# Block products for sixteen unit pairs of both FFNs, their weight sums made by accumulating transfers

## The chip, the cores and the metric

The kernel runs on one core of a Trainium2 chip. The metric is the device time of one execution in microseconds; three runs of the kernel before gave a median of 1001.37 us. A profile comes from one further execution of its own, traced by the hardware profiler.

## What is computed

One decoder layer on a sequence of 512 tokens with 1024 features: a half-step SwiGLU FFN, a token mixer (eight stick-breaking heads and eight forgetting-attention heads), and a second half-step SwiGLU FFN. Each is normed, and shifted, scaled and gated by columns that come from the vector c. Cut to what matters here (everything is float32):

```
mod = silu(c) @ w_mod + b_mod            # nine vectors of 1024: shift, scale, gate of each sub-layer
h = rms_norm(x, g1) * (1 + sc1) + sh1
x = x + 0.5 * (1 + ga1) * ((silu(h @ w1_gate) * (h @ w1_up)) @ w1_down)     # D_FF = 2816
x = x + (1 + ga2) * hybrid_mixer(...)
h = rms_norm(x, g2) * (1 + sc3) + sh3
x = x + 0.5 * (1 + ga3) * ((silu(h @ w2_gate) * (h @ w2_up)) @ w2_down)
```

## The kernel before

Everything is held transposed: features on the 128 partitions, the 512 tokens along the free dimension. x is eight tiles of 128x512, h likewise. Matmuls run in fp32r on operands that are split in two: a high part (a cast, on ACT, `hi`) and the rest (a subtraction, on VectorE, `lo`). A product of a 128x128 weight block with an activation tile takes three matmuls (`mm3`): high by high, high by low, low by high.

**The FFN.** D_FF is 22 units of 128. A plain unit has a gate and an up projection, each of eight 128x128 blocks, so 24 matmuls of 512 columns into one PSUM bank. `gated` makes silu(gate) * up from them and splits it into `ah` and `al`. The units come in three parts (`FPARTS`, 8, 7 and 7); after each part `down` multiplies the part's activations with eight chunks of the down weights (bank `pt`) and `update` adds the gated result to x. Weights go through `prep`: a transfer on SyncE's queue into a `raw` slot (4 slots of 512 KB), the cast into `hi` (4 slots), the subtraction into `lo` (4 slots). A slot of hi or lo comes free when the product that reads it is done, so the split of one operand can run when the product four earlier has ended.

**The block pair** (`block_pair`). For seven pairs of neighbouring units of the second FFN (`SPLIT2`) the gate and up projections of two units are taken as one 2x2 block matrix product in the Strassen-Winograd form: seven products of half-size blocks in place of eight. The host stores the four quarter blocks (d11, d12, d21, d22, each 128x1024) of a pair one after another. Each product has 24 matmuls of 256 columns: two halves of four blocks by three. Four of the seven weight operands are sums of quarter blocks:

```
s1 = d21 + d22      s2 = s1 - d11      s3 = d11 - d21      s4 = d12 - s2
```

VectorE makes them from the raw tiles into `bsum` tiles (L458), and they are split like the others (L452, L453). The matching sums of h are made once (`block_sums`, L418 to L440): four of 256 tokens wide for each pair of h tiles, split into `th` and `tl`. The results are put together by VectorE (`result`, L480) in `bres` tiles (6 slots); the first product stays in its bank and is also copied out by ACT (L486). The order of the products is d11, s2, s1, d12, s3, s4, d22. Three banks are used: `o` for d11 and d12, `mm` and `z` for the rest.

**The modulation columns.** The 72 columns of 128 come from chunks of 128x1024 of w_mod, read into `wm` tiles (4 slots). VectorE multiplies a chunk with c and sums it into one column of `mods` (L215), and then adds the bias column (L218). The first 16 are made at the start. The other 56 are queued: `mod_next` takes two after each of the units 4 to 7 of the first FFN, three after each later one, and one after each down chunk.

**The end of the first FFN.** In the last part, five down chunks are done in full, `SumSq` collects the squares of x on GpSimd (L625), and three chunks are held back, split into `bw` tiles of their own, for `turn`, which finishes x and makes the next h in two halves of the tokens so that TensorE goes on.

**The order of the work.** Apart from stretches that are written out by hand (the start, and TensorE's order around the two turns), each engine's queue is put in order when the program is built, from the order of the code as priority and from estimated durations; at run time every queue is worked off in that order, SyncE's queue of loads included. A tile is handed out from the slots of its tag, and a load or an operation that writes it waits until the last reader of the slot's tile before is done. GpSimd issues no transfers. Outside of the turns its queue in the two FFNs is empty.

## Time and profile before

| | |
|---|---|
| runs, median (lowest) | 1001.37 us (1000.51 us) |
| the profiled execution's own time | 1001.51 us |
| its span, first to last instruction | 999.6 us |
| granted TensorE clock | 0.998 |
| TensorE / weight loads / VectorE / ACT / GpSimd busy | 984.3 / 847.7 / 666.4 / 401.8 / 117.9 us |
| read from HBM | 125.92 MB |

The stages, by the lines in the trace: the start and the first four units until about 60 us, the first FFN until its turn at some 370 us, the mixer until 645 us, the second FFN to the end. The block pairs stand between 680.3 and 936 us.

A row of a group or of the timeline names the line of the code, the engine, the operation and the tiles (out<-in, buffer numbers left out). In the timeline a row begins with its start and its duration. PEld is the loading of weights, which overlaps PE. What an engine waited for stands as `waiting line <- engine and line that released it`. TensorE pipelines its matmuls, so the distance of two starts, and not the duration, tells how fast they follow each other.

### The profile page before, as it was taken

The numbers are of one execution on the slowest core, as the hardware profiler recorded it, in microseconds if no ns is written. First come the engines' busy times: TensorE is split into PE (matmuls) and PEld (weight loads), VectorE is DVE, ScalarE is ACT, GpSimd is POOL, SyncE is SP. The second block draws the span as 40 slices with busy tenths as digits, with TensorE's granted clock in tenths as the row PEclk, the third lists the DMA queues.
The fourth block names the chain that finished last, engine by engine and source line by source line (L and its number), as shares of the span: only waits on it lengthen the run. The fifth ranks groups of instructions, "written<-read, shape, count | busy, mean of one in ns | idle before, by whom it ended". The sixth has DMA issues, their size and how long they took to land.

```text
span 999.6 us, 14256 instructions
## 1 busy us (share of the span) xinstructions
PE 984.3 (98%) x5648; PEld 847.7 (85%) x5648; DVE 666.4 (67%) x1042; ACT 401.8 (40%) x628; POOL 117.9 (12%) x131
## 2 busy tenths in 40 slices
PE   8999999999999999998999999999999999999998
PEld 7888788888888899877887867999988999899987
DVE  7999988524333437688767686699755678467532
ACT  6342222322223326587557462465431445134420
POOL 2000000000000033065413335110000000000000
PEclk9999999999999999999999999999999999999999
DMA  9888899432222402311111111213242224323321
GB/s 362 317 299 326 319 336 330 148 93 103 105 92 88 138 16 92 127 64 43 64 64 64 43 44 64 85 62 118 84 140 85 85 85 130 103 85 106 114 87 52
DMA packets 37362, 128.94 MB, mean 129 GB/s; under 512 B 4400, under 2 KB 4656, under 8 KB 37296
## 3 DMA queue, kind: packets, MB, share of 16 engines
q1 hardware_dynamic: 35712, 125.88, 36.4%
q10 hardware_dynamic: 1584, 2.16, 0.6%
q8 instruction: 44, 0.72, 0.3%
q14 instruction: 22, 0.18, 0.1%
HBM read 125.92 MB, written 2.10 MB: 128 GB/s over the span
## 4 chain that ended last, share of the span: by engine, by line
PE 81%; DVE 9%; issue 3%; ACT 3%; DMA 3%; POOL 1%; SPq 0%; ACTq 0%; DVEq 0%; POOLq 0%
PE mm L129 8%; PE pt L130 7%; PE pt L131 7%; PE pt L129 7%; PE mm L130 7%; PE mm L131 7%; PE z L131 4%; PE z L130 4%; PE z L129 4%; PE mm L475 2%; PE mm L474 2%; PE mm L473 2%; DMA wm<-wmod 2%; PE o L1019 2%; PE mm L401 1%
## 5 line engine op out<-in xcount | busy, mean ns | idle before, releaser
L124 ACT CAST hi<-raw 128x1024 fp32r<-128x1024 f32 (+2 forms) x126 | 129.1, 1027 | 287.0 <-PE pt L130 105.1
L125 DVE TENSOR_TENSOR lo<-raw,hi 128x1024 fp32r<-128x1024 f32 (+2 forms) x125 | 151.6, 1214 | 74.4 <-ACT hi L124 72.0
L129 PE MATMUL mm<-hh,hi 128*128 128x512 f32 (+1 forms) x352 | 136.1, 387 | 0.0
L130 PE MATMUL mm<-hl,hi 128*128 128x512 f32 (+1 forms) x352 | 134.1, 381 | 0.1
L131 PE MATMUL mm<-hh,lo 128*128 128x512 f32 (+1 forms) x352 | 134.0, 381 | 0.0
L130 PE MATMUL pt<-al,hi 128*128 128x512 f32 (+1 forms) x331 | 128.2, 387 | 0.6 <-DVE al L414 0.6
L129 PE MATMUL pt<-ah,hi 128*128 128x512 f32 (+1 forms) x331 | 128.1, 387 | 0.0
L131 PE MATMUL pt<-ah,lo 128*128 128x512 f32 (+1 forms) x331 | 128.0, 387 | 0.0
L569 DVE SCALAR_TENSOR_TENSOR x<-pt,gcol,x 128x512 f32<-128x512 f32 (+1 forms) x51 | 36.3, 712 | 100.0 <-PE pt L131 99.9
L130 PE MATMUL z<-hl,hi 128*128 128x512 f32 (+1 forms) x224 | 83.7, 374 | 0.0
L131 PE MATMUL z<-hh,lo 128*128 128x512 f32 (+1 forms) x224 | 83.7, 374 | 0.0
L129 PE MATMUL z<-hh,hi 128*128 128x512 f32 (+1 forms) x224 | 83.7, 374 | 0.0
L129 PEld LDWEIGHTS mm<-hh,hi 128*128 128x128 f32 x352 | 66.5, 189 | 13.8 <-issue 2.2
L131 PEld LDWEIGHTS mm<-hh,lo 128*128 128x128 f32 x352 | 66.4, 189 | 12.9
L130 PEld LDWEIGHTS mm<-hl,hi 128*128 128x128 f32 x352 | 66.5, 189 | 12.3 <-DVE hl L169 0.3
L215 DVE SCALAR_TENSOR_TENSOR junk<-wm,c_bc 128x1024 f32<-128x1024 f32 x56 | 68.3, 1219 | 11.8 <-DMA wm<-wmod 11.7
L130 PEld LDWEIGHTS pt<-al,hi 128*128 128x128 f32 x331 | 62.2, 188 | 13.6 <-DVE al L414 0.9
L129 PEld LDWEIGHTS pt<-ah,hi 128*128 128x128 f32 x331 | 62.2, 188 | 12.8 <-ACT ah L413 0.2
L131 PEld LDWEIGHTS pt<-ah,lo 128*128 128x128 f32 x331 | 62.2, 188 | 12.5
L625 POOL TENSOR_TENSOR sqp<-x 128x512 f32<-128x512 f32 x10 | 11.3, 1134 | 351.5 <-DVE x L569 351.5
L410 DVE TENSOR_TENSOR av<-sg,z 128x512 f32<-128x512 f32 x27 | 18.5, 685 | 48.8 <-PE z L131 48.8
L130 PEld LDWEIGHTS z<-hl,hi 128*128 128x128 f32 x224 | 42.2, 188 | 7.5
(349 smaller groups left out, 2159.6 us busy)
## 6 DMA issues: line engine op xcount, KB each, us to landing
raw<-w SPq DMA_DIRECT2D x80, 512.0 KB, 3.6
wm<-wmod SPq DMA_DIRECT2D x72, 512.0 KB, 5.8
raw<-wqk SPq DMA_DIRECT2D x16, 512.0 KB, 3.6
raw<-w1d SPq DMA_DIRECT2D x16, 448.0 KB, 3.2
raw<-w2d SPq DMA_DIRECT2D x16, 448.0 KB, 3.3
raw<-w1s SPq DMA_DIRECT2D x8, 512.0 KB, 5.7
raw<-w1d SPq DMA_DIRECT2D x8, 512.0 KB, 5.2
raw<-wo SPq DMA_DIRECT2D x8, 512.0 KB, 3.4
```

What stands on the lines that cost most here:

```text
L124: nc.scalar.copy(hi, raw)
L125: (lo_engine or nc.vector).tensor_tensor(lo, raw, hi.bitcast(F32), op=ALU.subtract)
L129: nc.tensor.matmul(ps, lh, rh, start=first, stop=False)
L130: nc.tensor.matmul(ps, lh, rl, start=False, stop=False)
L131: nc.tensor.matmul(ps, ll, rh, start=False, stop=last)
L215: nc.vector.scalar_tensor_tensor(out=junk, in0=wm, scalar=1.0, in1=c_bc, op0=ALU.mult, op1=ALU.mult, accum_out=mods[:, i : i + 1])
L410: nc.vector.tensor_tensor(av[:, sl], sg[:, sl], u, op=ALU.mult)
L473: nc.tensor.matmul(b[:, sl], lh, rh, start=f, stop=False, skip_group_check=True)
L474: nc.tensor.matmul(b[:, sl], lh, rl, start=False, stop=False, skip_group_check=True)
L475: nc.tensor.matmul(b[:, sl], ll, rh, start=False, stop=e, skip_group_check=True)
L569: nc.vector.scalar_tensor_tensor(out=x[e][:, sl], in0=ps[:, sl], scalar=g_col(gm)[:, e : e + 1], in1=x[e][:, sl], op0=ALU.mult, op1=ALU.add)
L1019: nc.tensor.matmul(ob[g * 64 : g * 64 + 64, i * P : (i + 1) * P], V[:, i + j, (2 * p + g) * 64 : (2 * p + g + 1) * 64], pts[g][0][:, at + ...
```

## The change

- **More pairs.** `SPLIT2` is now every second unit from 4 to 20 (nine pairs), and the first FFN gets `SPLIT1`, every second unit from 8 to 20 (seven pairs), its weights stored by the host in the same way. `FPARTS` becomes 8, 8, 6, so that no pair straddles two parts. In the first FFN `block_sums` is called after the first part.
- **Sums by transfers.** The four sums of weight blocks are made by transfers that GpSimd issues and that add what they bring to what lies in the destination. s1 is d21 loaded and d22 added. s2 and s3 change their signs: ACT writes the negated tile (of s1, and of d11), and a transfer adds d11 or d21 from HBM, so they are d11 - s1 and d21 - d11. The fourth is made in the buffer of d12, once d12 has been split for its own product: s2 is added to it, from SBUF. So d11, d21 and d22 are each read twice.
- **Signs and order.** `block_sums` forms its second and third sum with the opposite sign. The order of the products becomes d11, s1, s2, d12, s3, s4, d22.
- **Buffers.** The negated tiles take slots of `wm`, which they share with the modulation chunks and with `block_sums`. `th` and `tl`, the squares at the start and the weights held back for `turn` share eight tiles `tb0` to `tb7`. `bres` has 4 slots, and `SumSq`, `turn` and the start of the first FFN take their tiles from it too.
- **Modulation columns.** The bias is added once for eight columns. `mod_next` takes one chunk after a pair of the first FFN and two after each down chunk.

The core of the diff:

```diff
-FPARTS = (8, 7, 7)
-SPLIT2 = (3, 6, 8, 11, 13, 15, 18)
+FPARTS = (8, 8, 6)
+SPLIT1 = tuple(range(8, NF, 2))
+SPLIT2 = tuple(range(4, NF, 2))
...
-        nc.vector.tensor_tensor(mods[:, i : i + 1], mods[:, i : i + 1], cols[:, i : i + 1], op=ALU.add)
...
             if d < KD - 1:
                 continue
+            nc.vector.tensor_tensor(mod_col(m), mod_col(m), cols[:, m * KD : (m + 1) * KD], op=ALU.add)
...
     def block_tile(tmp):
-        return tmp.tile([P, 2 * S], F32, tag="bsum", name=nm("bsum"), bufs=3)
+        return tmp.tile([P, 2 * S], F32, tag="wm", name=nm("bsum"), bufs=4)
...
-            nc.vector.tensor_tensor(t3, b1, a1, op=ALU.subtract)
-            nc.vector.tensor_tensor(t2, t3, a0, op=ALU.add)
-            nc.vector.tensor_tensor(t4, b0, t2, op=ALU.subtract)
-            hi = tmp.tile([P, 2 * S], F32R, tag=f"th{k}", name=nm("th"), bufs=1)
-            lo = tmp.tile([P, 2 * S], F32R, tag=f"tl{k}", name=nm("tl"), bufs=1)
+            nc.vector.tensor_tensor(t3, a1, b1, op=ALU.subtract)
+            nc.vector.tensor_tensor(t2, t3, a0, op=ALU.subtract)
+            nc.vector.tensor_tensor(t4, b0, t2, op=ALU.add)
+            hi = tmp.tile([P, 2 * S], F32R, tag=f"tb{2 * k}", name=nm("th"), bufs=1)
+            lo = tmp.tile([P, 2 * S], F32R, tag=f"tb{2 * k + 1}", name=nm("tl"), bufs=1)
...
     def block_pair(w, n_w, j, T, tmp):
-        raws = []
-        for n in range(4):
+        d11, d12, d21, d22 = (w[n_w + n] for n in range(4))
+
+        def load(src):
             raw = wpool.tile([P, 2 * S], F32, tag="raw", name=nm("raw"), bufs=4)
-            nc.sync.dma_start(raw, w[n_w + n])
-            raws.append(raw)
-        r11, r12, r21, r22 = raws
+            nc.sync.dma_start(raw, src)
+            return raw
+
+        def add_in(dst, src):
+            nc.gpsimd.dma_start(dst, src, accum_op=ALU.add)
+
+        def negated(src, other):
+            t = block_tile(tmp)
+            nc.scalar.mul(t, src, -1.0)
+            add_in(t, other)
+            return t
+
+        s1 = load(d21)
+        add_in(s1, d22)
+        r11 = load(d11)
...
-        def combined(x0, x1, op):
-            t = block_tile(tmp)
-            nc.vector.tensor_tensor(t, x0, x1, op=op)
-            return t
...
-                out = tmp.tile([P, S], F32, tag="bres", name=nm("bres"), bufs=6)
+                out = tmp.tile([P, S], F32, tag="bres", name=nm("bres"), bufs=4)
...
         bx, by, bz = bank("o"), bank("mm"), bank("z")
-        product(bx, parts(r11), whole_h(0, H0), True, True)
-        p1 = tmp.tile([P, S], F32, tag="bres", name=nm("bres"), bufs=6)
+        s2 = negated(s1, d11)
+        s3 = negated(r11, d21)
+        w11 = parts(r11)
+        r12 = load(d12)
+        r22 = load(d22)
+        product(bx, w11, whole_h(0, H0), True, True)
+        p1 = tmp.tile([P, S], F32, tag="bres", name=nm("bres"), bufs=4)
         nc.scalar.copy(p1, bx)
-        s1 = combined(r21, r22, ALU.add)
-        s2 = combined(s1, r11, ALU.subtract)
+        product(bz, parts(s1), summed_h(0), True, True)
+        r = result(bz, p1)
         product(by, parts(s2), summed_h(1), True, True)
         q = result(by, p1)
-        product(bz, parts(s1), summed_h(0), True, True)
-        r = result(bz, p1)
-        product(bx, parts(r12), whole_h(4, H0), False, True)
-        s3 = combined(r11, r21, ALU.subtract)
+        w12 = parts(r12)
+        add_in(r12, s2)
+        product(bx, w12, whole_h(4, H0), False, True)
         product(by, parts(s3), summed_h(2), False, True)
         c22 = result(by, r, r)
-        s4 = combined(r12, s2, ALU.subtract)
-        product(bz, parts(s4), whole_h(4, H1), False, True)
+        product(bz, parts(r12), whole_h(4, H1), False, True)
...
                     a += block_pair(w, n_w, j, blocks["T"], tmp)
                     n_w += 4
                     j += 1
+                    if startup:
+                        mod_next(1)
                     continue
...
+            if startup and part == 0:
+                blocks["T"] = block_sums(tmp)
...
             update(e, ps, gm, FULL)
-            mod_next(1)
+            mod_next(2)
...
-    finish = ffn(False, w1, w1d, 2, True, (4, 3), tmp)
+    finish = ffn(False, w1, w1d, 2, True, (4, 3), tmp, split=SPLIT1)
...
-    w1 = gu(get("w1_gate"), get("w1_up"))
+    w1 = gu(get("w1_gate"), get("w1_up"), SPLIT1)
```

The rest renames buffers: the squares at the start and turn's three split weights move to `tb0` to `tb7`, and `tmps(tmp)` becomes `tmps(tmp, "bres", 4)` in three places.

More of the change, by code (lines that the diff above doesn't have):

```diff
@@ L303, in shift_out @@
             nc.vector.tensor_tensor(mods[:, d : d + 1], mods[:, d : d + 1], cols[:, d : d + 1], op=ALU.add)
-        sqs = [tmp.tile([P, S], F32, tag="bw", name=nm("sq"), bufs=6) for _ in range(6)]
+        sqs = [tmp.tile([P, S], F32, tag=f"tb{n}", name=nm("sq"), bufs=1) for n in range(6)]
         sqs += [tmp.tile([P, S], F32, tag=t, name=nm("sq"), bufs=2) for t in ("sg", "av")]
         rs = tmp.tile([P, S], F32, tag="rs", name="rs1", bufs=1)
-        us = [tmps(tmp)("rsq", 256) for _ in range(2)]
+        us = [tmps(tmp, "bres", 4)("rsq", 256) for _ in range(2)]
         ms = [kb[7], kb[5]]
-        G, SH, tm = g_col(1), mod_col(0), tmps(tmp)
+        G, SH, tm = g_col(1), mod_col(0), tmps(tmp, "bres", 4)
         def add(a, b, sl=slice(0, S)):
@@ L574, in down @@
         nfull = KD if boundary is None else KD - 1 if boundary == "end" else KD - NB
-        acc = SumSq(tmps(tmp)) if boundary not in (None, "end") else None
+        acc = SumSq(tmps(tmp, "bres", 4)) if boundary not in (None, "end") else None
         def steps(wt, ps, sl):
@@ L607, in down @@
         elif boundary:
+            spare = iter(range(2 * NB))
             def split():
-                return [tmp.tile([P, nf * P], F32R, tag="bw", name=nm("bw"), bufs=6) for _ in range(2)]
+                return [
+                    tmp.tile([P, nf * P], F32R, tag=f"tb{next(spare)}", name=nm("bw"), bufs=1) for _ in range(2)
+                ]
             ws = {e: prep(chunk(e), nf * P, split=split) for e in range(nfull, KD)}
-            return turn(ws, steps, gm, acc.acc, boundary, tmps(tmp))
+            return turn(ws, steps, gm, acc.acc, boundary, tmps(tmp, "bres", 4))
     NB = 3
```

## The prediction

> **What bounds the kernel now.** I read the page's shares and slices first, then the table of stretches, then TensorE's waits.
>
> ```profile
> span 999.6 us, 14256 instructions
> PE 984.3 (98%) x5648; PEld 847.7 (85%) x5648; DVE 666.4 (67%) x1042; ACT 401.8 (40%) x628; POOL 117.9 (12%) x131
> PE   8999999999999999998999999999999999999998
> PEclk9999999999999999999999999999999999999999
> ...
> 50.00:100.00 50.00, 50.00 (x222) 41.42 (x221) 47.48 (x89) 18.39 (x26) 0.00 (x0) 1.00 0.88 313
> ...
> 200.00:250.00 50.00, 50.00 (x223) 41.39 (x222) 17.85 (x22) 12.46 (x15) 0.00 (x0) 1.00 0.30 98
> ...
> PE z L944 <- ACT fw L104: 2.1, 1, 2.1
> ...
> PE pt L130 <- DVE al L414: 0.6, 1, 0.6
> ```
>
> TensorE is busy in every slice, at full clock, in both FFNs and in the mixer. Its longest named wait is 2.1 us, in the mixer; in an FFN it is 0.6 us, at the end of a part, where the down projection waits for the last activation's low part. The stretch columns after the span are PE, PEld, DVE, ACT, POOL, clock, DMA share and GB/s. So the time of an FFN is the number of matmuls by the spacing of their starts, and an edit pays only through these. Busy durations overlap (TensorE pipelines), so the price of a matmul is read from starts, in the order of time:
>
> ```profile
> 800.94 0.39 PE L129 MATMUL z<-hh,hi 128*128 128x512 f32 x1
> ...
> 806.38 0.28 PE L473 MATMUL o<-hh,hi 128*128 128x256 f32 x1
> ...
> 826.53 0.28 PE L473 MATMUL o<-hh,hi 128*128 128x256 f32 x1
> ...
> 846.69 0.40 PE L129 MATMUL pt<-ah,hi 128*128 128x512 f32 x1
> ```
>
> From 800.94 to 806.38 run the 24 matmuls of 512 columns of one plain projection (8 blocks by 3): 5.44 us, 0.2267 each. From 806.38 to 846.69 run two block pairs, 2 x 168 matmuls of 256 columns: 40.31 us, 0.1200 each. Half the columns cost 53%, not 50%, and this takes most of the algebra's gain.
>
> **The sum.** A pair of plain units is 4 projections of 24: 96 x 0.2267 = 21.76 us. A block pair is 7 products of 24 half-width matmuls: 168 x 0.1200 = 20.16 us. It saves 1.60 us. The change has 7 + 9 = 16 pairs where there were 7, so 9 new ones: 9 x 1.60 = 14.4 us. The other matmuls stay: three parts of 8, 8, 6 are again 22 steps for each output chunk.
>
> Against this stand the edits that must stay hidden.
>
> *Sums off VectorE.* In the pairs of before VectorE is nearly full:
>
> ```profile
> 680.30:700.50 20.20, 20.20 (x169) 20.12 (x168) 19.22 (x22) 11.67 (x15) 0.00 (x0) 1.00 0.44 153
> 826.50:846.70 20.20, 20.20 (x171) 20.20 (x170) 16.83 (x22) 10.12 (x15) 0.00 (x0) 1.00 0.45 137
> ...
> L458 DVE TENSOR_TENSOR bsum<-raw,raw 128x1024 f32<-128x1024 f32 x14 | 17.1, 1219 | 5.2 <-DMA raw<-w 5.2
> L453 DVE TENSOR_TENSOR lo<-bsum,hi 128x1024 fp32r<-128x1024 f32 x28 | 33.8, 1220 | 8.7 <-ACT hi L452 8.5
> L480 DVE TENSOR_TENSOR bres<-mm,bres 128x512 f32<-128x512 f32 x21 | 14.5, 688 | 7.0 <-PE mm L475 7.0
> L410 DVE TENSOR_TENSOR av<-sg,bres 128x256 f32<-128x256 f32 x21 | 8.8, 417 | 0.0
> L414 DVE TENSOR_TENSOR al<-av,ah 128x512 fp32r<-128x512 f32 x44 | 30.0, 684 | 1.6 <-ACT ah L413 1.6
> L452 ACT CAST hi<-bsum 128x1024 fp32r<-128x1024 f32 x28 | 29.1, 1050 | 41.8 <-PE pt L130 16.3 <-DVE bsum L458 9.0 <-PE o L474 8.8
> ```
>
> Per pair it now does 7 low parts at 1.22, 4 sums at 1.22, 5 results at 0.69, 4 half products at 0.42 and 2 low parts at 0.68: 19.9 us of 20.16. Without the 4 sums it is 15.0. ACT gets two negations; the nearest row is its cast of the same shape, 1.05, so 2.1 on top of some 11 us, 13 of 20.16. Neither engine is the bound, and these cost nothing while the queues keep moving. Were VectorE still to do the sums, it would have 0.3 us a pair in hand, less than one modulation chunk of 1.22 in FFN1.
>
> *Accumulating transfers.* No row of before shows one; POOL issues no DMA. Two prices are needed: the share of the DMA engines and the time from issue to landing. The nearest rows:
>
> ```profile
> raw<-w SPq DMA_DIRECT2D x80, 512.0 KB, 3.6
> wm<-wmod SPq DMA_DIRECT2D x72, 512.0 KB, 5.8
> ...
> 809.33 1.05 ACT L452 CAST hi<-bsum 128x1024 fp32r<-128x1024 f32 x1 [1.34 <-PE o L474]
> ```
>
> Share: between 200 and 250 us the engines were 0.30 busy for 98 GB/s: 15 us for 4.9 MB, or 1.60 us of all sixteen for a 512 KB tile. A pair has 4 plain loads and 4 accumulating ones; if one of these costs k tiles, the pair needs (4 + 4k) x 1.60 us. k = 1 gives 12.8. If the destination's read counts fully, k = 2 and it is 19.2, inside 20.16. Only above k = 2.15 are the DMA engines the bound. I take a value at or a little under 2.
>
> The Trainium skill bears on this: "Collectives: The Full Stack", The bandwidth ceiling, says that an add in the DMA path reads two sources through one ring and so delivers about half the rate of a copy. By it the pair needs 19.2 us; it gives the rival on the DMA engines below. No run here shows it yet.
>
> Landing: a plain tile lands in 3.6 us in quiet stretches (80 weight loads) and in 5.8 among the modulation loads. For an accumulating one I take 3.6 as the low bound, 2 x 5.8 = 11.6 as the high one and 2 x 3.6 = 7.2 as the value, since most pairs stand in stretches at a DMA share under a half. How much is there? The hi/lo ring has 4 slots: the cast at 809.33 waited for the end of the product that began at 806.38, three products before its own use. A product is 24 x 0.12 = 2.88 us and a split 1.05 + 1.22 = 2.3. The tightest chain is the fourth sum, which adds s2 into r12's own buffer: r12 is split for the fourth product, at the earliest as the pair's first product starts, ready 2.3 later; the sum must land 2.3 before the sixth product, at 5 x 2.88 - 2.3 = 12.1. That leaves 9.8 us, against 7.2. The chain of s1 (a load of 3.6, a transfer, a negation of 1.05, another transfer) has from 3.5 us before one pair's start to 23.6 after it: 27.1 - 4.7 = 22.4 for two transfers, 11.2 each. Behind the add of r12 on POOL's queue stands only the next pair's first add, and behind a negation on ACT the casts of the next products, with 8.64 - 2.3 = 6.3 us in hand. So at 7.2 nothing reaches TensorE. I take 0, with 0 to 1.8 us a pair as its bounds.
>
> *FFN1's block sums and the modulation chunks.* The sums of h are now made in FFN1 too: 4 x (2 x 0.68 + 4 x 0.41 + 1.22) = 17 us of VectorE, and they share four wm slots with the modulation loads.
>
> ```profile
> L215 DVE SCALAR_TENSOR_TENSOR junk<-wm,c_bc x56: 1211/1218/1228, 51.4 to 183.3; 128x1024 f32<-128x1024 f32 x56
> ...
> L218 DVE TENSOR_TENSOR mods<-mods,cols x56: 146/158/161, 56.6 to 184.6; 128x1 f32<-128x1 f32 x56
> ...
> L239 DVE TENSOR_SCALAR gcol<-mods x2: 167/170/172, 77.5 to 184.8; 128x8 f32<-128x8 f32 x2
> L160 DVE SCALAR_TENSOR_TENSOR ht<-x,gcol,hold x16: 468/472/479, 377.1 to 650.1; 128x256 f32<-128x256 f32 x16
> ...
> 148.84 0.39 PE L129 MATMUL mm<-hh,hi 128*128 128x512 f32 x1
> ```
>
> The first gate column is ready at 77.5 and comes before the block sums in the program; the next columns are first used at 377, and the chunks were through at 183.3. So 17 us more, and a slower loading beside the pairs, are covered by some 190 us; the 56 small adds that become 7 give 49 x 0.158 = 7.7 us back. Were that cover gone, up to 17 us would show. POOL's queue is empty in this stretch.
>
> *End of the last parts.* The last part now has 6 units and ends in a block pair, whose fifth and sixth activations the down projection wants sooner: the sixth low part at 5 x 0.68 + 0.23 = 3.6 us after the last product instead of 4.3. The pair of before that ended at 846.69 had it when?
>
> ```profile
> 846.89 0.69 DVE L480 TENSOR_TENSOR bres<-mm,bres 128x512 f32<-128x512 f32 x1 [0.56 <-PE mm L475]
> ...
> 849.52 0.68 DVE L414 TENSOR_TENSOR al<-av,ah 128x512 fp32r<-128x512 f32 x1
> ```
>
> At 850.20, 3.5 us after. So 0 to 0.6 us at each of two ends (0.6 is the wait named above); I take 1.0 for both. The buffers that changed names (bw and sq to tb, SumSq and turn to bres) are free by the time they are wanted: five chunks of 18 x 0.2267 = 4.1 us lie between the last use of the block sums and turn's products. Nothing for them.
>
> Sum: 1001.5 (this execution's own time; span 999.6 and 1.9 around it) - 14.4 + 1.0 = 988.1. The median of the runs is 1001.4, so 988.0.
>
> **The rivals.**
>
> *FFN1's second part becomes bound by DMA.* For: in FFN1 the DMA share is 0.88 at 50 to 100 us. At k = 2 the four pairs need 4 x 19.2 = 77 us, one pair of it prefetched through the four raw slots: 58. One modulation chunk comes every 131.9 / 55 = 2.4 us, so at 148.8 some 15 of 56 are left, 24.6 us of DMA; with 7 more held back by the block sums, 36. That is 82 to 94 us in the four pairs' 80.6. Loss 2 to 13, say 7: 995. Against: those loads may wait until the part is done, and a ring of four wm slots holds them back as soon as s2 and s3 sit in it.
>
> *Slower than before: the sum into r12 lands too late.* Its place is POOL's fourth add of every pair; nothing but that 9.8 us decides. If it lands in 11.6 us, the upper bound, the sixth product waits 1.8 us in each of 16 pairs: 29 us, 1017. From 9.8 + 13.4 / 16 = 10.6 us on the kernel is slower than before. For: the transfer can't start before both parts of r12 are split, it may queue behind another add, and SP's loads share the engines. Against: the quiet rows, 3.6 us.
>
> *TensorE's time doesn't follow the matmuls.* If the transfers cost k = 3, a pair needs 25.6 us of DMA, 5.4 too many; with the first pair of each of five groups prefetched, 11 x 5.4 = 60: 1048. No row speaks for it.
>
> **How the numbers follow.** Forecast 988, chance 0.58, its own range 985 to 992. DMA-bound second part, 995: 0.2. Late fourth sum, 1017: 0.16, spread over 1000 to 1030 with the landing time. k = 3 and the like: 0.05. Better than 984: 0.01; nothing in the sum has room for it. The range is 984 to 1012: it leaves out the upper part of the third case and the fourth, about 0.15. Two per cent, about what a measurement of this kernel can tell from no change, is 20 us: faster than 981.4 would need more than all 9 pairs give, 0.01; slower than 1021.4 takes the late sum near its bound or k = 3, 0.1; within, 0.89.
>
> **What would show it.** Matmuls of 256 columns in the products rise from 7 x 168 = 1176 to 2688, still 0.12 us apart, and 864 of 512 columns go. VectorE's sums of raw tiles are gone, busy in consecutive pairs about 15 of 20. The DMA share in the pairs rises to 0.6 to 0.95, and POOL's accumulating transfers land in 5 to 9 us. Modulation chunks run on past 183 us. TensorE names no wait on a split in a pair beyond a few tenths. The forecast is wrong if TensorE waits for o, z or mm products on an ACT cast or VectorE low part that itself waited for a transfer, or if a transfer lands later than 9.8 us.

## The result and the profile after

The changed kernel takes 1083.7 us (median of four runs, 1082.1 to 1090.1) where the kernel before took 1001.6 beside it: a ratio of 1.084, 95% interval 1.079 to 1.088. One of the four runs of the kernel before took 1963.0 us and is left out of the ratio. The forecast was 988.0, its range 984 to 1012. The change lost 82 us where the sum had a gain of 13.

First the page of the changed kernel: busy time by engine, TensorE and its clock in 40 slices, and the two kinds of DMA queue (packets, MB, share of sixteen engines).

```profile
span 1082.9 us, 15960 instructions
...
PE 999.8 (92%) x6284; PEld 890.1 (82%) x6284; DVE 703.4 (65%) x1083; ACT 467.6 (43%) x718; POOL 172.2 (16%) x195
...
PE   8999987879968998999999999997899987999798
...
PEclk9999998889988999999999999998899988999899
...
q1 hardware_dynamic: 35712, 125.88, 35.1%
q0 software_dynamic: 9216, 33.56, 17.5%
```

TensorE is no longer busy in every slice, and in the same slices, those of the block pairs, the granted clock is below full. Before, TensorE showed nines in all but three slices, and the clock in all. The queue q0 holds the 64 accumulating transfers: 17.5% of 1082.9 us is 189.5 us, 2.96 us of all sixteen engines for each 512 KB.

TensorE's own waits, and the waits of the queues that feed it (us in total, times, longest):

```profile
PE mm L482 <- ACT hi L466: 32.7, 6, 6.3
PE mm L482 <- DVE bres L489: 23.3, 5, 9.3
PE o L482 <- ACT bres L500: 5.5, 1, 5.5
```

```profile
POOL raw L451 <- DMA raw<-w: 141.7, 8, 28.1
...
POOL bsum L451 <- ACT bsum L455: 118.5, 23, 9.4
...
ACT bsum L455 <- DMA raw<-w: 92.4, 16, 13.9
...
ACT hi L466 <- DMA raw<-bsum: 80.8, 15, 9.0
```

Before, no wait in an FFN was over 0.6 us. Now twelve waits inside the pairs make 61.5 us, up to 9.3 each. The other rows give the chain behind them: ACT's negation (L455) waits for the transfer that makes s1, GpSimd's transfers (L451) wait for the negation, and ACT's cast of the fourth sum (L466) waits for `raw<-bsum`, the transfer that adds s2 into r12.

A stall costs more than its length. The table of stretches around the first one in FFN1 (start:end, length, busy of PE, PEld, DVE, ACT, POOL, then clock, DMA share, GB/s):

```profile
155.00:160.00 5.00, 4.65 (x39) 4.44 (x38) 1.64 (x2) 0.07 (x1) 0.87 (x1) 1.00 1.06 226
160.00:168.00 8.00, 0.02 (x1) 0.02 (x1) 3.04 (x5) 3.22 (x4) 0.00 (x0) 0.68 0.37 90
168.00:172.00 4.00, 4.00 (x19) 4.00 (x20) 2.53 (x3) 0.00 (x0) 0.00 (x0) 0.50 0.71 243
172.00:176.00 4.00, 4.00 (x31) 4.00 (x31) 2.25 (x3) 1.37 (x2) 0.83 (x1) 0.86 0.36 131
176.00:180.00 4.00, 4.00 (x36) 4.00 (x35) 3.09 (x5) 2.48 (x4) 0.04 (x1) 1.00 0.87 171
```

Two neighbouring starts lie 8.6 us apart here, and behind this gap the clock is 0.50 for about 5 us (0.50 in one whole window of 4 us, 0.86 over the next): 19 matmuls start in a window that later holds 36. The Trainium skill ("TensorE: Matmul & The Clock Gate", Part 1: The HAM clock gate) says that the rate is half after an idle window of about 3.4 us and full again after a busy window of the same length. The rows agree with both.

**The balance.** I take every start on TensorE from the timeline. Behind matmuls of 512 or 256 columns, from 10 us on, 17 neighbouring starts lie over 1 us apart, 75.6 us together (before: 3, 4.6 us). Where the next start comes sooner than that, but later than 0.2267 or 0.1200 us, 45.1 us are lost (before: 16.6). So -14.4 for the matmuls, +71.0 for the gaps, +28.5 for the slow starts: +85, against 82 measured. Inside the pairs it is 62 for the gaps and 24 for the slow starts. By pairs it shows in the starts too. One group of four pairs, FFN2's second part, from its first matmul to the first of the down projection:

```profile
836.60 0.28 PE L482 MATMUL o<-hh,hi 128*128 128x256 f32 x1
...
933.71 0.40 PE L130 MATMUL pt<-ah,hi 128*128 128x512 f32 x1
```

That is 97.1 us for four pairs, 24.3 each, where a pair of before took 20.16. From here on a group is counted from the start of its first matmul to that of its last, 0.12 us less. In the five groups (four and three pairs in FFN1, two, four and three in FFN2) a pair then takes 26.7, 26.7, 27.7, 24.2 and 22.9 us.

**One turn of the loop.** The rows below are one period in FFN2: GpSimd's issues, then ACT's operations that hang on them, then VectorE's.

```profile
862.78 0.86 POOL L451 DMA_DIRECT2D bsum<-w  x1 [5.94 <-ACT bsum L455]
863.67 0.87 POOL L451 DMA_DIRECT2D raw<-bsum  x1
864.21 1.22 POOL L451 DMA_DIRECT2D bsum<-w  x1
882.24 0.86 POOL L451 DMA_DIRECT2D raw<-w  x1 [16.80 <-DVE av L411]
891.40 0.86 POOL L451 DMA_DIRECT2D bsum<-w  x1 [8.30 <-ACT bsum L455]
892.00 1.16 POOL L451 DMA_DIRECT2D raw<-bsum  x1
```

```profile
871.07 2.94 ACT L466 CAST hi<-raw 128x1024 fp32r<-128x1024 f32 x3 [5.69 <-DMA raw<-bsum]
...
890.04 2.01 ACT L455 ACTIVATE bsum<-raw 128x1024 f32<-128x1024 f32 x2 [2.94 <-DMA raw<-w]
...
892.94 1.05 ACT L466 CAST hi<-bsum 128x1024 fp32r<-128x1024 f32 x1
900.11 2.94 ACT L466 CAST hi<-raw 128x1024 fp32r<-128x1024 f32 x3 [6.12 <-DMA raw<-bsum]
```

```profile
872.14 1.22 DVE L467 TENSOR_TENSOR lo<-raw,hi 128x1024 fp32r<-128x1024 f32 x1 [4.91 <-ACT hi L466]
873.29 0.68 DVE L489 TENSOR_TENSOR bres<-mm,bres 128x512 f32<-128x512 f32 x1
...
886.81 1.23 DVE L467 TENSOR_TENSOR lo<-raw,hi 128x1024 fp32r<-128x1024 f32 x1
...
902.33 0.68 DVE L489 TENSOR_TENSOR bres<-mm,bres 128x512 f32<-128x512 f32 x1
```

TensorE's matmuls at the pair's first start and at its gap, and the chain of work that ended last (start, length, what):

```profile
885.28 0.28 PE L482 MATMUL o<-hh,hi 128*128 128x256 f32 x1
...
896.68 0.28 PE L484 MATMUL o<-hh,lo 128*128 128x256 f32 x1
903.16 0.55 PE L482 MATMUL mm<-th,hi 128*128 128x256 f32 x1 [6.20 <-ACT hi L466]
```

```profile
863.67 7.29 DMA raw<-bsum
...
876.27 5.35 DMA raw<-w
...
892.00 8.01 DMA raw<-bsum
```

*One gap.* The pair's first product starts at 885.28. The low part of r12 is made at 886.81 and ends at 888.04: from here on the fourth sum could be added. Its transfer is issued at 892.00, because on GpSimd's queue a sum of the *next* pair stands ahead of it (891.40), which waits for a negation on ACT (890.04), which waits for a transfer: 4.0 us late. It lands at 900.0, 8.0 us after. ACT casts (900.11), VectorE makes the low part, and only behind this low part comes the result `q` (902.33 to 903.01), which the fifth product needs, since it goes on in the bank `mm`. That product was wanted at 896.80 and starts at 903.16, 0.15 after `q` ends. From the split to the wanted start are 8.8 us, of which cast, low part and `q` take 3.0: 5.8 are there for a transfer that takes 4.0 + 8.0, and the difference, 6.2, is the wait in TensorE's row. (The row names ACT's cast, because the third cast of the group at 900.11 ends at 903.05, nearly with `q`. But the product's own operand had been cast at 892.94, so the cast only looks like the releaser; `q` is what it needs. In two gaps of FFN1, at 159.4 and 312.7 us, the last cast had ended 1.2 us before the start, and the result on VectorE 0.06 us before it.)

*The round.* `raw<-bsum` at 863.67 is the fourth sum of the pair before. It lands at 870.97, and its split (from 871.07) sets the buffer of r12 free. The splits of two more tiles follow it on ACT and VectorE, and SyncE's queue, which works in order, goes on with loads as buffers come free, at 876.27 with d21 of the pair after next. That lands at 881.62, and GpSimd adds d22 to it at 882.24 (the row names VectorE's `av`, but in the sixteen pairs this issue follows the landing of the load by 0.6 to 0.8 us). This lands at 890.0, ACT negates, GpSimd issues a sum at 891.40 and, behind it, at 892.00, the fourth sum of the next pair. The loop is closed: 7.3 landing + 5.3 splits + 5.35 load + 0.6 issue + 7.8 landing + 2.0 negation and issue = 28.3 us from one `raw<-bsum` to the next, against 20.16 us of matmuls. The last pair of a group has no pair behind it, and no such gap.

### The profile page after: what moved, and what is told of

It is laid out like the page before. It is cut to its first block, busy times and chain, and to the rows that moved or that the text cites. A ratio compares the mean times of both kernels' runs of the same rounds, so it can differ in the third digit from the quotient of the medians.

```text
span 1082.9 us, 15960 instructions
## 1 busy us (share of the span) xinstructions
PE 999.8 (92%) x6284; PEld 890.1 (82%) x6284; DVE 703.4 (65%) x1083; ACT 467.6 (43%) x718; POOL 172.2 (16%) x195
## 3 DMA queue, kind: packets, MB, share of 16 engines
q1 hardware_dynamic: 35712, 125.88, 35.1%
q0 software_dynamic: 9216, 33.56, 17.5%
## 4 chain that ended last, share of the span: by engine, by line
PE 41%; DVE 7%; DMA 7%; ACT 4%; issue 4%; POOL 1%; POOLq 0%; ACTq 0%; DVEq 0%
PE pt L131 5%; PE pt L132 5%; PE pt L130 4%; DMA raw<-w 4%; PE mm L130 3%; PE mm L131 3%; PE mm L132 3%; DMA raw<-bsum 3%; PE mm L482 2%; PE mm L483 2%; PE mm L484 2%; PE o L1039 2%; PE z L964 1%; PE pt L1023 1%; PE z L484 1%
## 5 line engine op out<-in xcount | busy, mean ns | idle before, releaser
L482 PE MATMUL mm<-th,hi 128*128 128x256 f32 x384 | 119.0, 310 | 56.1 <-ACT hi L466 32.7
L467 DVE TENSOR_TENSOR lo<-raw,hi 128x1024 fp32r<-128x1024 f32 x80 | 97.2, 1222 | 93.8 <-ACT hi L466 92.8
L466 ACT CAST hi<-raw 128x1024 fp32r<-128x1024 f32 x80 | 81.7, 1047 | 160.1 <-DMA raw<-bsum 80.8
L482 PEld LDWEIGHTS mm<-th,hi 128*128 128x128 f32 x384 | 82.5, 215 | 58.4 <-ACT hi L466 33.8
L483 PE MATMUL mm<-tl,hi 128*128 128x256 f32 x384 | 117.1, 305 | 0.0
L484 PE MATMUL mm<-th,lo 128*128 128x256 f32 x384 | 116.7, 304 | 0.4 <-DVE lo L467 0.4
L484 PEld LDWEIGHTS mm<-th,lo 128*128 128x128 f32 x384 | 82.5, 215 | 0.6 <-DVE lo L467 0.6
L483 PEld LDWEIGHTS mm<-tl,hi 128*128 128x128 f32 x384 | 82.8, 216 | 0.0
L130 PE MATMUL mm<-hh,hi 128*128 128x512 f32 (+1 forms) x208 | 79.7, 383 | 0.0
L482 PE MATMUL o<-hh,hi 128*128 128x256 f32 x256 | 73.6, 288 | 5.5 <-ACT bres L500 5.5
L451 POOL DMA_DIRECT2D raw<-w x16 | 14.1, 880 | 377.1 <-DMA raw<-w 141.7
```

The lines of the kernel that those rows point to most:

```text
L130: nc.tensor.matmul(ps, lh, rh, start=first, stop=False)
L466: nc.scalar.copy(hi, src)
L467: nc.vector.tensor_tensor(lo, src, hi.bitcast(F32), op=ALU.subtract)
L482: nc.tensor.matmul(b[:, sl], lh, rh, start=f, stop=False, skip_group_check=True)
L483: nc.tensor.matmul(b[:, sl], lh, rl, start=False, stop=False, skip_group_check=True)
L484: nc.tensor.matmul(b[:, sl], ll, rh, start=False, stop=e, skip_group_check=True)
```

## Experiments

Nine of the kernels in one table, each timed with the kernel before beside it on the same chip. The columns in the middle are us per pair in the five groups, worked out from starts as above, first to last (in the last row, marked *, the parts hold 8, 6, 8 units and the groups 3, 4, 2, 3, 4 pairs); "excess" is the sum over the sixteen pairs of what lies over 20.16, and is 0.6 us too low in every row for that way of counting.

| kernel | FFN1 pairs | FFN2 pairs | excess | time | ratio to before, 95% |
|---|---|---|---|---|---|
| the change | 26.7, 26.7 | 27.7, 24.2, 22.9 | 85.6 | 1083.7 | 1.084 [1.079, 1.088] |
| GpSimd's order mended | 23.1, 23.4 | 20.5, 20.9, 20.6 | 26.2 | 1021.0 | 1.020 [1.018, 1.022] |
| and ACT's order | 23.3, 23.1 | 21.2, 22.2, 22.4 | 38.5 | 1034.6 | 1.034 [1.031, 1.036] |
| and `q` first on VectorE | 24.6, 24.2 | 20.2, 20.8, 20.5 | 33.8 | 1031.2 | 1.029 [1.027, 1.032] |
| fourth sum on VectorE | 24.1, 22.3 | 23.0, 20.4, 20.5 | 29.8 | 1026.0 | 1.025 [1.024, 1.027] |
| transfers copy only | 21.6, 21.3 | 21.0, 20.6, 20.6 | 14.0 | 1010.4 | 1.009 [1.006, 1.012] |
| order mended, copy only | 20.4, 20.8 | 20.1, 20.1, 20.1 | 2.5 | 1000.9 | 0.999 [0.998, 1.000] |
| all sums on VectorE | 20.1, 20.1 | 20.1, 20.2, 20.1 | -0.4 | 996.2 | 0.996 [0.994, 0.997] |
| the same, parts 8, 6, 8 * | 20.1, 20.1 | 20.1, 20.2, 20.2 | -0.1 | 990.7 | 0.989 [0.988, 0.991] |

Add the excess to the 996.2 us of the kernel with no excess, and you have the time of each of them but the last within 3 us: 996.2 + 85.6 = 1081.8 for the change, then 1022.4, 1034.7, 1030.0, 1026.0, 1010.2 and 998.7. The loss is in the pairs and hardly anywhere else.

**GpSimd's order mended.** A dependency of order alone puts every add of a pair behind the fourth sum of the pair before on GpSimd's queue; no data moves differently.

```diff
         def add_in(dst, src):
-            nc.gpsimd.dma_start(dst, src, accum_op=ALU.add)
+            i = nc.gpsimd.dma_start(dst, src, accum_op=ALU.add).ins
+            if behind["sum"]:
+                tc.add_manual_dep(i, behind["sum"].name, order, reason="add order")
+            return i
...
-        add_in(r12, s2)
+        behind["sum"] = add_in(r12, s2)
```

> Edit: on POOL's queue the adds of the next pair stand behind the fourth sum of the pair before; same transfers, same bytes. Theory 1 (the order of POOL's queue: the fourth sum stands behind the next pair's second add, which waits for a negation, which waits for a first add): TensorE's gaps of 5 to 9 us in the pairs go, and with them the half clock behind each; 985 to 1005 us. Theory 2 (the transfers themselves are too slow or take too much of the DMA engines): the fourth sum is late all the same, 1060 to 1085. Theory 3 (the negations wait on ACT's queue ahead of casts): most gaps stay, 1040 to 1075.

1021.0: 62.7 us of the 82 came back with an edge of order. The builder answered it on the other queues too: beside 24 of GpSimd's 195 instructions, 30 of ACT's 729 (negations that now stand behind casts are among them), 43 of VectorE's 1083 and 7 of SyncE's 248 stand elsewhere. So this run alone doesn't tell GpSimd's order from ACT's; the run with the fourth sum on VectorE, below, does. GpSimd's issues in two turns in FFN1, and TensorE's waits that are left:

```profile
174.32 0.87 POOL L453 DMA_DIRECT2D raw<-bsum  x1 [10.95 <-DVE lo L472]
174.87 1.21 POOL L453 DMA_DIRECT2D raw<-w  x1
183.62 0.87 POOL L453 DMA_DIRECT2D bsum<-w  x1 [7.54 <-ACT bsum L460]
...
196.20 0.88 POOL L453 DMA_DIRECT2D raw<-bsum  x1 [9.81 <-DVE lo L472]
```

```profile
PE mm L487 <- DVE bres L494: 16.6, 11, 2.9
```

The fourth sum now waits for VectorE's split of r12 alone, it lands in 4.6 us (median) where it took 7.3, and no gap in a pair is over 3.2 us, so that the clock is back at 0.993 in the mean. A rest of 26 us of excess stays, 21 of it in FFN1.

**ACT's order as well.** The negations of a pair stand behind the last cast of the pair before, because in the trace of the change they stand ahead of it on ACT and wait there for a transfer.

```diff
-            nc.scalar.mul(t, src, -1.0)
+            i = nc.scalar.mul(t, src, -1.0).ins
+            if behind["cast"]:
+                tc.add_manual_dep(i, behind["cast"].name, order, reason="add order")
...
+        behind["cast"] = cast["i"]
```

> Edit: as the first, and on ACT the two negations of the next pair stand behind the last cast of the pair before. Theory 1: no more than 5 us below the first edit, 985 to 1000 us. Theory 2: 1060 to 1085. Theory 3: here, and only here, the gaps go: 985 to 1005, at least 30 us below the first edit.

A miss: 1034.6, worse by 13.6 than without it. Only ACT's queue is in another order here. The negations now come later, and with them s2 and s3, whose transfers `bsum<-w` take 9.6 us to land where they took 8.0; the pairs of FFN2 go from 20.5 to 20.9 up to 21.2 to 22.4. So the later start of the negations cost more than the casts gained. ACT's order was not turned round without GpSimd's.

**The result `q` ahead of the fourth sum's low part on VectorE**, with GpSimd's order mended.

```diff
-        product(bz, parts(r12), whole_h(4, H1), False, True)
+        product(bz, parts(r12, q_ins), whole_h(4, H1), False, True)
```

(`parts` makes the low part depend on `q_ins` in order. The builder also puts some 60 of VectorE's 1083 instructions elsewhere.)

> Edit: the POOL order of the first experiment, and on VectorE the result q, which frees the bank of the fifth product, stands ahead of the low part of the fourth sum. In the first experiment TensorE waited 16.6 us in 11 places for q, and q waited behind that low part. If VectorE's order is the rest of the loss, these go with the half clock behind them: 998 to 1008 us. If the transfers' landing (7 to 8 us now) is the rest, the wait moves to the cast of the fourth sum, and the time stays at 1013 to 1022.

A miss as well: 1031.2, and TensorE still waits 22.7 us for results on VectorE. The trace of the run with GpSimd's order mended shows why: it is mostly another result that is late there, that of the fifth product (`c22`), which the seventh product needs in the same bank. VectorE in that run (the bank `mm` is wanted at 187.99 in this stretch, an FFN1 pair):

```profile
184.29 1.23 DVE L472 TENSOR_TENSOR lo<-raw,hi 128x1024 fp32r<-128x1024 f32 x1 [2.40 <-ACT hi L471]
186.19 1.23 DVE L472 TENSOR_TENSOR lo<-raw,hi 128x1024 fp32r<-128x1024 f32 x1 [0.67 <-ACT hi L471]
...
187.67 1.22 DVE L216 SCALAR_TENSOR_TENSOR junk<-wm,c_bc 128x1024 f32<-128x1024 f32 x1
...
188.81 0.69 DVE L494 TENSOR_TENSOR bres<-mm,bres 128x512 f32<-128x512 f32 x1
```

Two low parts that waited for casts, and a modulation chunk, stand ahead of it.

**The fourth sum by VectorE**, in place in r12's buffer; the other three stay transfers.

```diff
-        add_in(r12, s2)
+        nc.vector.tensor_tensor(r12, r12, s2, op=ALU.add)
```

> Edit: the fourth sum is made by VectorE in place (1.22 us a pair); the other three stay transfers, in the order that the program gets by itself. Theory 1: the entry that stood at the wrong place is gone from POOL, VectorE has 16.2 of 20.16 us a pair; 985 to 1005 us. Theory 2: three quarters of the transfers stay and most of the loss with them, 1040 to 1065. Theory 3: the negations still wait ahead of casts, 1040 to 1075.

1026.0. It takes the blocked transfer away instead of letting it pass, and gets back about as much (58 us) as the order did. Both undo the same thing: the fourth sum no longer stands behind the next pair's. Here ACT's queue is nearly that of the change (3 of 729 instructions stand elsewhere), and its negations wait 87.8 us for transfers, where they waited 92.4; so their place on ACT isn't what cost the 58 us.

**Copies in place of adds.** The order on GpSimd, ACT and VectorE is that of the change, instruction by instruction.

```diff
-            nc.gpsimd.dma_start(dst, src, accum_op=ALU.add)
+            nc.gpsimd.dma_start(dst, src)
```

> Edit: the transfers that POOL issues copy and don't add, all else as in the changed kernel, queue orders included; so the sums of weight blocks are left out (each holds only what came last). It prices the add. Theory 2 (the add's price: twice the share of the DMA engines, late landing): the share per 512 KB tile falls from 3.0 to about 1.6 us, landings from 5.5 to 7.3 to 4 to 5 us, and the time with them, to 1030 or less. Theory 1 (the order of the queues): each link of the loop gets 1.5 to 2.5 us shorter but the fourth sum still stands behind two of them, 1050 to 1075.

Landing by issue, first in the change, then with copies (KB, median us), and q0 of the second:

```profile
bsum<-w POOLq DMA_DIRECT2D x32, 512.0 KB, 6.0
...
raw<-w POOLq DMA_DIRECT2D x16, 512.0 KB, 5.5
raw<-bsum POOLq DMA_DIRECT2D x16, 512.0 KB, 7.3
```

```profile
q0 software_dynamic: 9216, 33.56, 9.9%
...
bsum<-w POOLq DMA_DIRECT2D x32, 512.0 KB, 4.3
...
raw<-w POOLq DMA_DIRECT2D x16, 512.0 KB, 4.2
raw<-bsum POOLq DMA_DIRECT2D x16, 512.0 KB, 3.5
```

9.9% of 1007.5 us over 64 transfers is 1.56 us of sixteen engines for a tile, 2.96 with the add. So the copies are cheaper in two ways, in landing time and in the engines' share, and this run can't tell them apart. In the loop, 7.3 and 7.8 for the two landings become 3.5 and 4.2: 28.3 - 7.4 = 20.9 us, and the pairs take 20.6 to 21.6. In one gap the sum is issued 4.0 late and lands in 3.5, so 7.5 stand against the 5.8 that are there, which leaves 1.7; the gaps in the pairs of this run are 1.2 to 2.6. So the bad order with quick landings keeps only 14 of the 86 us. Most of the loss needs both the order and the price of the adds.

**Order mended and copies.**

> POOL's order mended and the transfers copy in place of adding (the sums are left out), the same order on every engine as in the run of POOL's order. If the order and the landing time of the adds are the two halves of one loop, both mended leave little: pairs of FFN2 at 20.2 to 20.4, of FFN1 at 20.5 to 21, and the time is 996 to 1002, of which 6 is the short last part of FFN1. If the loss of the run with copies alone (1010) had other causes, it stays at about 1010.

1000.9, with pairs at 20.1 in FFN2 and at 20.4 and 20.8 in FFN1: nothing is left in the pairs but 2.5 us. The order and the price of the adds (landing and share) are together nearly the whole of the excess.

**All four sums on VectorE**, sixteen pairs, no transfers that add, no negated tiles, each quarter block read once.

```diff
-        s1 = load(d21)
-        add_in(s1, d22)
-        r11 = load(d11)
+        r21, r22, r11 = load(d21), load(d22), load(d11)
+        s1 = block_tile(tmp)
+        nc.vector.tensor_tensor(s1, r21, r22, op=ALU.add)
...
-            nc.scalar.mul(t, src, -1.0)
-            add_in(t, other)
+            nc.vector.tensor_tensor(t, other, src, op=ALU.subtract)
```

> Edit: all four sums by VectorE, sixteen pairs, no accumulating transfer, no negation on ACT. By the prediction's count VectorE then has 19.9 of 20.16 us a pair in runs of two to four pairs. If that count is right and decides, TensorE waits for low parts and results in the second and later pairs, some 1 to 3 us each, and FFN1 with its modulation chunks more: 995 to 1025 us. If VectorE catches up in the down projections and starts overlap as its rows do (1.14 instead of 1.22 apart), 986 to 994. The three theories of the transfers all expect less than 1030.

996.2, and every pair at 20.1 to 20.2. So VectorE, counted at 19.9 of 20.16 us a pair, was not a bound: starts on it lie closer than durations (in the changed kernel a low part of 1.22 us at 872.14 is followed by the next start at 873.29, 1.15 later). In FFN2's four pairs it is busy 17.1 us a pair, and 18.7 in FFN1's four, where the modulation chunks found room too. What is left against the forecast lies at the end of FFN1, in TensorE's waits:

```profile
PE mm L731 <- ACT hh L167: 2.8, 1, 2.8
PE pt L130 <- ACT ah L414: 2.5, 1, 2.5
```

The second is the start of the last part's down projection, the first the turn's new h; in the starts the gaps are 2.8, 3.1 and 1.2 us. Neither was there before.

**The same with parts of 8, 6 and 8 units.** The short part stands in the middle; pairs still don't straddle.

```diff
-FPARTS = (8, 8, 6)
+FPARTS = (8, 6, 8)
```

> Edit: all four sums by VectorE, and the parts 8, 6, 8 in place of 8, 8, 6. With all sums on VectorE the kernel stood at 996.2, 8 us over the sum of the prediction; TensorE waited 2.5 us at the end of the first FFN's last part and 3.7 us at its turn. Eight units in the last part give turn's held-back chunks 8 x 3 x 6 x 0.12 = 17.3 us of TensorE's work in place of 13.0, and the last activation 1.4 us more. If the short last part is the cause: 989 to 992. If the shared buffers of turn are: 995 to 997.

990.7, the fastest kernel of the study (0.989 of before, interval 0.988 to 0.991); the three gaps shrink to one of 1.3 us. The gain of 5.5 us is what the short last part cost in this kernel.

**That edit with GpSimd's order mended** and the transfers kept:

> POOL's order mended and FFN parts of 8, 6, 8 units in place of 8, 8, 6. With VectorE's sums this change of parts was worth 5.5 us (996.2 to 990.7). If that is the end of the short last part and the start of the turn, it is worth the same here: 1013 to 1017. If the gain was due to VectorE's load, 1021 stays.

A miss: 1022.7, no gain. The gaps at the end of FFN1 do shrink, from 3.0, 3.1 and 1.2 us to one of 1.9, and the excess in the pairs fell to 21.0, but TensorE now waits in the first short down projection, where the bank of a chunk is read late by VectorE, behind a modulation chunk whose load came late:

```profile
PE pt L130 <- DVE x L590: 6.9, 2, 3.8
```

```profile
254.02 1.23 DVE L216 SCALAR_TENSOR_TENSOR junk<-wm,c_bc 128x1024 f32<-128x1024 f32 x1 [6.65 <-DMA wm<-wmod]
```

With sums on VectorE no such wait was there, so the gain of the edit depends on what else the queues hold.

**The sums on VectorE, parts of 8, 6, 8, and three modulation chunks after a down chunk** in place of two:

```diff
-            mod_next(2)
+            mod_next(3)
```

> Edit: as the one with parts 8, 6, 8, and three modulation chunks after each down chunk, so that all 56 are through before the last part. At the end of the last part the low part of the last activation stood behind modulation chunks on VectorE. If these chunks take a share in the wait: 1 to 3 us below the one with parts 8, 6, 8. If the wait is the length of the chain alone: the same within 0.5 us.

A miss: 996.1, slower than the 990.7 without it. The pairs of FFN1's third part go from 20.1 to 21.3, with one stall of 3 us where the first pair's low part on VectorE is late. Chunks taken in bursts cost more here than they gave at the end of the last part.

**Why FFN1's pairs stay 3 us too long with the order mended.** Three runs, all with GpSimd's order mended, each taking something of the modulation chunks away. In the first the chunks multiply a tile that is there in place of their load; in the second they load and multiply 64 of their 1024 columns; in the third none comes after a pair.

```diff
-            mod_chunk(m, d)
+            mod_chunk(m, d, c_bc)
```

> The adds of a pair stand behind the fourth sum of the pair before, as in the run of POOL's order (1021), and the 56 queued modulation chunks multiply the resident c tile in place of a chunk of w_mod, so that their loads are left out (wrong modulation columns) and their tiles take no slot of wm. Theory 1, FFN1's seven pairs are 3 us too long there because the modulation loads take the DMA engines beside the accumulating transfers: pairs of FFN1 at 20.5 to 21, time about 1003. Theory 2, the seven pairs are long for the queues' order alone: pairs stay at 23, time 1018 to 1022.

```diff
+            nc.sync.dma_start(wm[:, :64], wmod[m, d][:, :64])
...
+                out=junk[:, :64], in0=wm[:, :64], scalar=1.0, in1=c_bc[:, :64], op0=ALU.mult, op1=ALU.mult,
```

> As the run without the modulation loads, but each queued chunk loads and multiplies 64 of its 1024 columns (wrong modulation columns): the wm tiles are still taken in the old order, nearly without DMA traffic. If the traffic is the cause of FFN1's 3 us a pair, the pairs are as in the run without the loads, about 20.5 to 21, time about 1003. If it is the sharing of the four wm slots between chunks and negated tiles, the pairs stay near 23 and the time near 1018, while the run without the loads falls.

```diff
-                    if startup:
-                        mod_next(1)
...
-            mod_next(2)
+            mod_next(3)
```

> POOL's order mended, no modulation chunk after a pair of FFN1, three after a down chunk in place of two. In the run of POOL's order FFN1's pairs took 23.1 to 23.4 us and FFN2's 20.5 to 20.9, and it was not the traffic of the modulation loads. Theory 1, the chunk of 1.22 us that VectorE works off ahead of a result (once in a pair, behind the late low part) holds the bank mm: FFN1's pairs fall to 20.5 to 21.5 and the time to 1004 to 1012. Theory 2, it is the wm slots that chunks hold while a negated tile waits for one: the pairs fall as far, and the negations on ACT come earlier after the casts. Theory 3, it is the start of the part, whose first pairs' loads stand behind those of the down projection: the pairs stay at 23, the time at 1021.

| order mended, and | FFN1 pairs | FFN2 pairs | time | ratio, 95% |
|---|---|---|---|---|
| nothing else | 23.1, 23.4 | 20.5, 20.9, 20.6 | 1021.0 | 1.020 [1.018, 1.022] |
| no chunk loads, no wm slots | 23.9, 20.8 | 20.2, 20.5, 21.0 | 1014.0 | 1.013 [1.011, 1.014] |
| loads of 64 columns, slots kept | 22.9, 22.9 | 20.1, 20.9, 21.0 | 1019.7 | 1.019 [1.017, 1.020] |
| no chunk after a pair | 24.6, 20.6 | 20.5, 20.8, 20.8 | 1019.5 | 1.018 [1.016, 1.020] |

The traffic of the chunks is not the cause: with nearly all of it gone and the slots kept, both groups stay at 22.9. The third part is quick, at 20.6 to 20.8, in the first and the last of the three runs, where no chunk there takes a slot or is loaded. That fits the wm slots that chunks and negated tiles share, but the runs don't show it alone: with loads of 64 columns VectorE still waits for chunks in the third part, 8.0 us in three places, up to 5.4 with a low part behind it, and this wait is gone in the other two as well. In the second part none of the three helps (22.9 to 24.6), only dropping the adds does (20.4); the DMA engines aren't full in it, since without the chunk loads their share falls from 0.84 to 0.66 and its pairs take 23.9. Why that group, and not the four of FFN2's second part, stays open.

## Why the prediction was wrong

**The step that failed** is in the accumulating transfers: "Behind the add of r12 on POOL's queue stands only the next pair's first add". I asked who stands behind this add and not who stands ahead of it. Ahead of it stand the next pair's first and second add; the second waits for ACT's negation, that for the landing of the first, and that for a load that SyncE's queue can't issue before the fourth sum of the pair before has been split. The queue is put in order when the program is built, and nothing in the text of `block_pair`, where the fourth sum stands before the next pair, decides it. In the turn above that made the add 4.0 us late. The runs show it from both sides: mend the order, and 62.7 us come back; make the transfers copies, which land sooner and take less of the engines, and 73.3 come back; do both, and the excess is 2.5. The term of the sum that rested on this step, "I take 0, with 0 to 1.8 us a pair", measured 5.4 us a pair.

**The landing time was right and its allowance was not.** 7.2 was taken for the fourth sum, and its median is 7.3. But the 9.8 us of "the tightest chain" ran to the sixth product. The fifth was the tight one: it needs `q`, and `q` stands on VectorE behind the low part of the fourth sum. In the turn above the allowance was 5.8. So 7.3 alone would have cost some 1.5 us a pair by this estimate, even with the add issued in time, had it stayed at that; it fell to 4.6 once it was issued apart from the others. The rival "the sum into r12 lands too late" had the right place and sign with the wrong mechanism: it priced a slow transfer at 1.8 us a pair, not one issued late in a closed round, at 2.7 to 7.6.

**The allowance for s1 was counted on an open chain.** "11.2 each" took s1's load as free to start early. In the loop the load comes only behind the split of another pair's fourth sum, so its two transfers and the fourth sum's landing add up in series.

**The share of the DMA engines was right.** k was taken at or a little under 2; it is 2.96 / 1.58 = 1.87, with 1.58 from q1 (35.1% of 1082.9 us for 125.88 MB). So the pair needs (4 + 4 x 1.87) x 1.58 = 18.1 us, and over the five groups the engines were 0.59 to 0.73 busy. The Trainium skill ("Collectives: The Full Stack", The bandwidth ceiling) says that an add in the DMA path reads two sources and so halves the rate; the 1.87 agrees with this. The rival with k = 3 is out. The rival of FFN1's second part by DMA is out for the loads of the chunks, since without them that part is no quicker. (Its sum priced a chunk at 1.64 us where the share gives 1.60; its loss then starts at 1.4 us and not at 2.)

**Half clock had no term.** The forecast priced a stall at its own length. Slow starts cost 28 of the 82 us, 24 of them inside the pairs, 0.4 us for each us of gap there.

**The nine pairs' 14.4 us were right.** With all sums on VectorE a pair takes 20.1 to 20.2 us in every group, and the kernel with the parts in the better order stands at 990.7, 2.7 above the forecast that this term carries.

**"Neither engine is the bound" was right, its ground too narrow.** VectorE would not have been the bound with the sums either. The room of "less than one modulation chunk" was worked out from durations, where starts are closer, and the chunks fitted in.

**The ends of the last parts were mis-sized**: 1.0 us for both. The run with parts of 8, 6, 8 shows 5.5, at the end of FFN1, where the kernel with parts of 8, 8, 6 had gaps of 2.8 at the down projection's start and 4.3 in the turn. The term looked at the sixth low part and had none for the turn, where a new h on ACT is late behind a shorter down projection.

**"Behind a negation on ACT" 6.3 us in hand** was wrong in the same way: it counted the negation as 1.05 us of work, and it is 1.05 us of work behind a wait of 92.4 us in 16 cases, with the casts of the pair at hand behind it. Turning that order round on top of GpSimd's did not help either: s2 and s3 then come later.

## What to carry to other kernels

When an edit adds a step that waits to an in-order queue, write down what stands *ahead* of each step in the order that was built, not only behind it, and follow each wait back until it reaches either a finished load or the step itself; if it reaches the step, the period is at least the sum of the whole round, whatever the shares of the engines say. A count of engine time with room left says nothing against such a round. Price a stall of more than a few microseconds on TensorE with the half clock after it, and before moving work off an engine that looks full, count its starts and not its durations.

## What the hardware showed besides

- An accumulating transfer of 512 KB takes 2.96 us of the sixteen engines against 1.56 for a copy on the same queue, and lands in 5.5 to 7.3 us against 3.5 to 4.3 (medians by issue).
- Landing goes with what was issued beside it: `raw<-bsum` takes 7.3 to 8.0 us in the change where it is issued between two other adds within 1.5 us, and 4.4 to 5.2 in the last pair of each group, where no add is issued beside it. It takes 4.6 with GpSimd's order mended, where `bsum<-w` goes from 6.0 to 8.0 instead (medians).
- The granted clock is 0.50 for about 5 us behind a gap of 8.6. With GpSimd's order mended, it is 0.50 for 3.4 us soon after a gap of 3.2 in a pair, but stays full behind one of 3.1 in the turn; its mean over that run is 0.993.
